# Sample selection of a two-layer hybrid decoder: row counts summed by a group matmul, and digits that carry the bias

## The chip, the cores and the metric

The kernel runs on one core of a Trainium2 chip. The core has five engines, each with an instruction queue of its own that it works through in the order in which it was written: PE (matrix multiplication; its weight loads are shown apart as PEld), DVE (vector), ACT (activation functions), POOL (a second vector engine, which also issues indirect transfers), and SP, which here only issues DMA transfers. Engines wait for one another by semaphores. SBUF is the on-chip memory of 128 partitions; PSUM is the memory into which PE writes its results, split into banks. The metric is the time of one execution on the device, in microseconds (us).

## What is computed

Two decoder layers run on a prompt of 1024 tokens and on 8 sample sequences of 4 new tokens with 2048 past keys each. In each layer one input projection feeds four groups of heads (a recurrent block, differential attention, sparse attention called DSA, and gated linear attention called GLA); an output projection and a gated MLP follow. The change is in DSA, in the choice of the 256 best-scored keys of each of the 32 sample tokens:

```python
def dsa_select(iq, iw, ik, q_pos, k_pos, topk):
    sc = jnp.einsum("bqhd,bsd->bqhs", iq, ik).astype(jnp.float32) * IDX_DIM ** -0.5
    score = jnp.einsum("bqh,bqhs->bqs", iw.astype(jnp.float32) * IDX_HEADS ** -0.5, jax.nn.relu(sc))
    score = jnp.where(k_pos[None, :] <= q_pos[:, None], score, -jnp.inf)
    val, idx = lax.top_k(score, topk)          # topk = 256
    return idx, jnp.isfinite(val)
```

## The kernel before, in words

The program is written layer by layer. A scheduler takes the instructions in the order in which the code emits them, simulates when they would run, and lays down one queue for each engine. On the chip these queues aren't reordered.

The stages of a layer that matter here are three. In the **dense stage** PE makes the input projections (L478) while DVE makes the threshold search of the prompt's own top-k (L833 to L906, tiles `tku`, `tkb`, `mk`). Then comes the **prelude** of GLA: a transfer brings the tile `ga`, PE multiplies it (L1823), ACT applies functions (L1824 to L1829), DVE makes a scan (L1830 to L1839) and the level tiles `gl` (L1885 to L1897), after which PE begins L1796. The **GLA stage** follows, with the differential attention of the samples (L1369, L1376, L1399) mixed in. DSA of the samples comes only behind it.

`sample_select()` finds, for each of 32 sample tokens, the 256th largest of 2176 scores. The scores of a token lie in four rows (partitions) of the tile `ss`, 128 rows of 544. The search fixes a threshold bit by bit. One **round** of it is: ACT applies Sign to all scores minus the candidate, and sums each row into `scnt` (L1017, an activation and a read of its accumulator); `group()` adds the counts of a token's four rows; DVE compares the sum with the number wanted (`sdf`, L1062), updates the threshold `sth` (L1063) and makes the next bias `snc` from it (L1059). There are 15 rounds on the upper 16 bits (`sdl`, L1037 to L1042), then `digits(15)` with 16 rounds on the lower bits, then `digits(12)` with 13 rounds on the position of equal scores; with three plain counts made by DVE (L1010) that makes 47 sums by `group()` in a layer. Between the two calls of `digits` a table is loaded by DMA (L1074) and combined with the scores (L1076).

The code is a generator. Each of its steps is emitted by others: in the dense stage by `background()`, once for each tile of a projection, in the GLA stage once for each second step of the GLA generator, and what is left by `samples()` before DSA:

```python
            while advance(ggen):
                n += KA
                count[0] += 1
                if count[0] % SELM == 0:
                    advance(sel)
                advance(sgen, int(n))
...
                while kind == "dsa" and advance(sel):
                    yield
```

PSUM is shared out by stage. `banks(**PSH)`, with PSH = dict(d=2,m=2,s=2), opens the banks of the dense stage; `banks(**PSG)` at L1748, with PSG = dict(d=2,e=1,g=5), closes `m` and `s` and opens `e` and `g` where they stood. `bank("m")` takes the next buffer of a tag. A tile in a bank that was another's waits until that one's readers are done.

Of the kernel before, what the change touches and what calls it, by code (L numbers as in the profile page):

```python
# [10 lines left out]
F32 = mybir.dt.float32  # L11
# [6 lines left out]
OP = mybir.AluOpType  # L18
# [53 lines left out]
def _const_tables():  # L72

    p = np.arange(128)
    c = {}
# [29 lines left out]
    pb, pj, pt = p // 16, (p // 4) % 4, p % 4  # L105
    bb, jj = np.arange(32) // 4, np.arange(32) % 4
    c["tailbad"] = ~((pj[:, None] == 3) & (pb[:, None] == bb[None, :]) & (jj[None, :] <= pt[:, None]))
    r = np.arange(32)
    c["agrp"] = ((p[:, None] % 32) // 16 == r[None, :] // 16) & (pt[:, None] == r[None, :] % 4)
    c["emat"] = np.concatenate([(pb[:, None] == b) & (pj[:, None] == p[None, :] // 32) & (pt[:, None] == p[None, :] % 4)  # L110
                                for b in range(8)], 1)
    c["newmask"] = np.concatenate([np.where((bb[None, :] == b) & (jj[None, :] <= pt[:, None]), 0.0, NEG)
# [3 lines left out]
    g, pp = np.arange(512) // 128, np.arange(512) % 128  # L116
# [18 lines left out]


CONST, COFF = _const_tables()


@with_exitstack  # L140
def trunk(ctx, tc, io, out, dbg=None, depth=DEPTH, stop=99):
    nc = tc.nc
    dve, act, pool, pe, sp = nc.vector, nc.scalar, nc.gpsimd, nc.tensor, nc.sync
    mult, add, sub = OP.mult, OP.add, OP.subtract
# [4 lines left out]
    psum = []  # L149

    def bank(tag="d"):
        pool_, bufs = psum[0 if tag in "de" else 1][:2]
        return pool_.tile([128, 512], F32, tag=tag, name=tag, bufs=bufs[tag])
# [62 lines left out]
    def const(key, dt=F32, where=None, parts=128, side="left"):  # L216
        o, w = COFF[key]
        t = (where or cp).tile([parts, w], dt, name="c_" + key, bufs=1)
        if dt == F32:
            sp.dma_start(t, cin[:parts, o:o + w])  # L220
        else:
            with tc.tile_pool(reuse_waits="tile", name="cs", bufs=1, side=side) as cs:
                s = cs.tile([parts, w], F32, name="cs_" + key)
                sp.dma_start(s, cin[:parts, o:o + w])
                pool.tensor_copy(t, s)
        return t
# [326 lines left out]
    with tc.tile_pool(reuse_waits="tile", name="xin", bufs=9) as xi:  # L553
# [6 lines left out]
        pc = bank("m")  # L560
        for k in range(8):
            pe.transpose(pc[:, 9 * k:9 * k + 9], c9[:, k * 128:k * 128 + 128], ident[:9, :9])
        th = xi.tile([128, 72], F32, name="th", bufs=1)
# [3 lines left out]
        for i, (t0, n) in enumerate(TOK):  # L567
            xn = xi.tile([128, D], F32, name="xn")
            sp.dma_start(xn[:n, :], xf_p[t0:t0 + 128, :] if i < 8 else xf_s)
            for q in range(2):  # L570
                pc = bank("d")
# [38 lines left out]
    pt = io["page_table"]  # L610
# [30 lines left out]
    for l in range(depth):  # L641
# [351 lines left out]
        def sample_select():  # L993
# [3 lines left out]

            def group(cnt):

                rep_ = kp.tile([128, 32], F32, name="srep", bufs=2)  # L1000
                dve.transpose(rep_, cnt.to_broadcast([128, 32]))
                pc = kp.tile([128, 1], F32, name="spc", bufs=2)
                dve.tensor_tensor_reduce(out=rep_, in0=rep_, in1=agrp, scale=1.0, scalar=0.0, op0=mult, op1=add,
                                         accum_out=pc)
                return pc

            def group_count(src, thr, op):

                cnt = kp.tile([128, 1], F32, name="scnt", bufs=2)
                dve.tensor_scalar(scs, src, thr, None, op0=op, op1=add, accum_out=cnt)  # L1010
                yield
                return group(cnt)

            def group_signs(src, bias, scale):

                cnt = kp.tile([128, 1], F32, name="scnt", bufs=2)
                act.activation(scs, src, AF.Sign, bias=bias, scale=scale, accum_out=cnt)  # L1017
                for _ in range(GY):
                    yield
                return group(cnt)  # L1020
# [7 lines left out]
            pc = yield from group_count(ss, 0.0, OP.is_ge)  # L1028
# [6 lines left out]
            for bit in range(30, 15, -1):  # L1035
                nc_ = kp.tile([128, 1], F32, name="snc", bufs=2)
                dve.tensor_scalar(nc_, cf, -1.0, cap[:, 0:1], op0=mult, op1=OP.min)  # L1037
                pc = yield from group_signs(hi16, nc_[:, 0:1], ng[:, 1:2])
                d = kp.tile([128, 1], I32, name="sdl", bufs=2)
                dve.tensor_scalar(d, pc, float(2 * TOPK - NS), float(1 << bit), op0=OP.is_lt, op1=mult)  # L1040
                dve.scalar_tensor_tensor(cs_, d, (1 << (bit - 1)) if bit > 16 else 0, cs_, op0=OP.bitwise_xor,
                                         op1=OP.bitwise_xor)  # L1042
            dve.tensor_scalar(cs_, cs_, -65536, None, op0=OP.bitwise_and)
            pc = yield from group_count(hi16, cf, OP.is_gt)
            need = kp.tile([128, 1], F32, name="sneed", bufs=1)
# [6 lines left out]
            th = kp.tile([128, 1], F32, name="sth", bufs=1)  # L1052
            dve.memset(th, 0.0)

            def digits(bits, need):

                for bit in range(bits, -1, -1):
                    nc_ = kp.tile([128, 1], F32, name="snc", bufs=2)
                    dve.tensor_scalar(nc_, th, -1.0, 0.5 - float(1 << bit), op0=mult, op1=add)  # L1059
                    pc = yield from group_signs(ev_, nc_[:, 0:1], 1.0)  # L1060
                    d = kp.tile([128, 1], F32, name="sdf", bufs=2)
                    dve.tensor_scalar(d, pc, need[:, 0:1], float(1 << bit), op0=OP.is_ge, op1=mult)  # L1062
                    dve.tensor_tensor(th, th, d, op=add)  # L1063

            yield from digits(15, need)
            lo = kp.tile([128, 1], I32, name="slo", bufs=1)
            dve.tensor_scalar(lo, th, ng[:, 2:3], ng[:, 3:4], op0=mult, op1=add)
            dve.tensor_tensor(cs_, cs_, lo, op=OP.bitwise_or)
            thr = cf
            pc = yield from group_count(ss, thr, OP.is_gt)  # L1070
# [138 lines left out]
        kp = kpool.__enter__()  # L1209
# [3 lines left out]
        agrp = const("agrp", where=kp)  # L1213
# [941 lines left out]
        if True:  # L2155
# [58 lines left out]
            for q in range(11):  # L2214
# [27 lines left out]
                for j in range(2):  # L2242
# [19 lines left out]
                    th = G[:, :T]  # L2262
# [99 lines left out]
```

## Time and profile before

| | us |
|---|---|
| median of 3 runs (lowest, highest) | 3806.49 (3804.55, 3810.34) |
| the profiled execution | 3821.09 |
| its span, first to last instruction | 3819.3 |
| mean granted clock of TensorE in it | 0.956 |

The profile shows one execution. A share of busy time is a mean over all stages: PE is busy for 91% of the span and DVE for 64%, but the search is in use only from 377 to 684 us in layer 0 and from 2255 to 2550 us in layer 1, so it is the stretches there that are to be read, one by one.

### The profile page before, as it was taken

The page shows a single profiled execution, that of the slowest core. Times are in us where ns is not written, and L with a number is a line of the kernel's source. Part 1 is how long each engine was busy: PE and PEld are TensorE (multiplying, and loading weights), DVE is VectorE, ACT ScalarE, POOL GpSimd, SP SyncE. Part 2 cuts the span into 40 slices and gives each one's busy share as a digit, 9 for nine tenths or more (in the row PEclk, how much of TensorE's full clock was granted, in tenths as well). Part 3 has the DMA queues.
Part 4 walks back from the last instruction along what each step waited for, and adds up shares of the span by engine and source line. Part 5 has one row for each costly group of instructions (what it writes and reads, how often), then busy time and mean ns, then how long its engine had stood idle before and what let it go on. Part 6 is the DMA issues. An engine that isn't in the chain of part 4 may idle for free.

```text
span 3819.3 us, 64298 instructions
## 1 busy us (share of the span) xinstructions
PE 3494.2 (91%) x24916; PEld 3125.7 (82%) x24916; DVE 2452.0 (64%) x5724; ACT 1500.7 (39%) x3026; POOL 1271.7 (33%) x1179
## 2 busy tenths in 40 slices
PE   7999868899899999999989988588997999999998
PEld 4888855576699999999979877356666999999997
DVE  5479998677554444455564999986763645555555
ACT  4445643476532121212244557436663322122122
POOL 2134146534333222222322521654333233222231
PEclk8999979999999999999989999699998999999999
DMA  6453345646511432321123332456455011111111
GB/s 232 136 158 107 96 125 167 204 144 206 181 44 49 116 103 73 94 78 45 45 83 95 104 96 70 135 177 201 154 170 175 28 40 56 45 45 45 45 51 52
DMA packets 351404, 407.64 MB, mean 107 GB/s; under 512 B 93712, under 2 KB 299262, under 8 KB 349915
## 3 DMA queue, kind: packets, MB, share of 16 engines
q1 hardware_dynamic: 312186, 265.09, 23.0%
q0 software_dynamic: 38912, 138.43, 10.9%
q8 instruction: 197, 3.23, 0.4%
q14 instruction: 109, 0.89, 0.1%
HBM read 354.32 MB, written 58.04 MB: 108 GB/s over the span
## 4 chain that ended last, share of the span: by engine, by line
PE 68%; DVE 19%; DMA 4%; issue 4%; ACT 3%; POOL 1%; SPq 1%; another core or an unknown queue 0%; DVEq 0%; ACTq 0%; POOLq 0%
PE d L478 31%; PE m L2180 13%; PE d L498 4%; PE d L1369 3%; DVE tku L833 3%; DVE tkb L833 2%; PE e L1399 2%; PE e L1376 1%; PE m L1637 1%; PE d L330 1%; PE m L1696 1%; DVE ny L413 1%; PE g L1796 1%; PE m L753 1%; PE m L1689 1%
## 5 line engine op out<-in xcount | busy, mean ns | idle before, releaser
L478 PE MATMUL d<-h,wh 128*128 128x384 f32 (+1 forms) x5856 | 1405.7, 326 | 52.4 <-ACT h L468 15.7
L478 PEld LDWEIGHTS d<-h,wh 128*128 128x128 f32 x5856 | 1030.3, 190 | 67.7 <-ACT te L706 16.2
L478 PE MATMUL d<-h,wl 128*128 128x384 f32 (+1 forms) x2928 | 945.2, 325 | 8.5 <-POOL wl L462 8.5
L478 PEld LDWEIGHTS d<-h,wl 128*128 128x128 f32 x2928 | 556.4, 190 | 13.4 <-POOL wl L462 12.0
L498 PE MATMUL d<-wh,h 128*128 128x256 f32 (+1 forms) x2304 | 450.3, 291 | 34.3 <-ACT nat L697 16.1
L507 DVE SCALAR_TENSOR_TENSOR xT<-m,mod,xT 128x384 f32<-128x384 f32 (+1 forms) x480 | 273.1, 572 | 228.7 <-PE m L2180 227.8
L498 PEld LDWEIGHTS d<-wh,h 128*128 128x128 f32 (+1 forms) x2304 | 360.3, 186 | 56.3 <-ACT nat L697 19.6
L462 POOL TENSOR_TENSOR wl<-wr,wh 128x1024 fp32r<-128x1024 f32 (+1 forms) x124 | 259.8, 2112 | 310.3 <-ACT wh L461 244.3
L2180 PE MATMUL m<-mh,wdh 128*128 128x384 f32 (+1 forms) x1056 | 350.4, 332 | 0.4 <-DVE xT L507 0.4
L2180 PE MATMUL m<-ml,wdh 128*128 128x384 f32 (+1 forms) x1056 | 344.0, 326 | 0.0
L2180 PE MATMUL m<-mh,wdl 128*128 128x384 f32 (+1 forms) x1056 | 341.9, 325 | 0.0
L498 PE MATMUL d<-wl,h 128*128 128x256 f32 (+1 forms) x1152 | 333.5, 290 | 3.1 <-DVE wl L462 2.0
L2279 POOL TENSOR_TENSOR ml<-z,mh 128x384 fp32r<-128x384 f32 x132 | 132.9, 1026 | 599.8 <-ACT mh L2278 599.8
L461 ACT CAST wh<-wr 128x1024 fp32r<-128x1024 f32 (+1 forms) x172 | 158.2, 956 | 210.7 <-PE d L478 172.3
L2250 DVE COPY fs<-G 128x2 f32<-128x2 f32 x44 | 50.8, 1156 | 278.4 <-ACT G L2230 278.4
L2230 ACT COPY G<-d 128x384 f32<-128x384 f32 x132 | 57.3, 442 | 421.6 <-PE d L478 393.8
L498 PEld LDWEIGHTS d<-wl,h 128*128 128x128 f32 (+1 forms) x1152 | 214.5, 186 | 7.7 <-issue 2.6
L2180 PEld LDWEIGHTS m<-mh,wdh 128*128 128x128 f32 x1056 | 200.0, 189 | 9.1 <-issue 6.7
L2180 PEld LDWEIGHTS m<-ml,wdh 128*128 128x128 f32 x1056 | 200.2, 190 | 1.4 <-issue 0.9
L2180 PEld LDWEIGHTS m<-mh,wdl 128*128 128x128 f32 x1056 | 200.0, 189 | 0.0
L2170 POOL TENSOR_TENSOR wdl<-wr,wdh 128x1024 fp32r<-128x1024 f32 x44 | 104.9, 2416 | 263.9 <-ACT wdh L2169 263.9
L1369 PE MATMUL d<-c_ident,kv 128*128 128x128 f32 x1024 | 167.0, 291 | 16.3 <-ACT KT L210 7.7
(556 smaller groups left out, 6600.2 us busy)
## 6 DMA issues: line engine op xcount, KB each, us to landing
adaw<-in_w_ada_dram SPq DMA_DIRECT2D x80, 512.0 KB
wr<-in_w_in_dram SPq DMA_DIRECT2D x48, 512.0 KB
wr<-in_ffn_w_gate_dram SPq DMA_DIRECT2D x44, 512.0 KB
wr<-in_ffn_w_up_dram SPq DMA_DIRECT2D x44, 512.0 KB
wr<-in_ffn_w_down_dram SPq DMA_DIRECT2D x44, 512.0 KB
xd<-xT SPq DMA_DIRECT2D x16, 528.0 KB
adaw<-in_w_ada_dram SPq DMA_DIRECT2D x8, 1024.0 KB
wr<-in_w_out_dram SPq DMA_DIRECT2D x32, 256.0 KB
```

Source lines behind the costliest of these rows:

```text
L461: act.copy(hi[:, ks, :width], raw[:, :, :width])
L462: eng.tensor_tensor(lo[:, ks, :width], raw[:, :, :width], hi[:, ks, :width].bitcast(F32), op=sub)
L478: pe.matmul(pd, lhsT=w[a][:, k, j * 128:j * 128 + 128], rhs=h[b][c][:, k, :], start=(q == 0), stop=(q == 23))
L498: pe.matmul(pd[:n, :256], lhsT=h[b][c][:, k, t0:t0 + n], rhs=w[a][:, k, :], start=(q == 0), stop=(q == 23))
L507: dve.scalar_tensor_tensor(x[:, m, t0:t0 + n], p[:, :n], mod[:, gate + m, 0:1], x[:, m, t0:t0 + n], op0=mult, op1=add)
L833: dve.tensor_scalar(scratch[:, :n], src[:, s], thr[:, j:j + 1], None, op0=OP.is_ge, op1=add, accum_out=cnt[:, j:j + 1])
L1369: pe.transpose(pm[:, z_ * 128:z_ * 128 + 128], kg[:, j, f * 128:f * 128 + 128], ident)
L1399: pe.matmul(po[32 * j:32 * j + 32, :256], lhsT=wT[:, g, 32 * j:32 * j + 32], rhs=vg[:, j, :], start=(g == 0), stop=(g == 3))
L2170: pool.tensor_tensor(lo[:, z_, :], raw, hi[:, z_, :].bitcast(F32), op=sub)
L2180: pe.matmul(pd, lhsT=a, rhs=b, start=(n == 0), stop=(n == len(ops) - 1))
L2230: act.copy(Gp[:, 2 + CHK[c][0]:2 + CHK[c][0] + n], p[:, :n])
L2279: pool.tensor_tensor(ml[:, cs], z[:, cs], mh[:, cs].bitcast(F32), op=sub)
```

## The change

`group()` no longer transposes the counts and reduces them under a mask on DVE; PE multiplies the counts `scnt` by a 128x128 matrix of zeros and ones (`agrp`, which grows from 32 to 128 columns) into a PSUM bank, tag `m` while the dense stage's banks are open, else `g`. The comparisons read the sum from PSUM. In `digits` the bias itself is carried from round to round: `sdf` and a scalar_tensor_tensor that writes the next `snc`, two DVE operations instead of three; the threshold `sth` is made from it once at the end. The rounds on the upper bits (L1036 to L1042) keep their three operations.

```diff
     bb, jj = np.arange(32) // 4, np.arange(32) % 4
     c["tailbad"] = ~((pj[:, None] == 3) & (pb[:, None] == bb[None, :]) & (jj[None, :] <= pt[:, None]))
     r = np.arange(32)
-    c["agrp"] = ((p[:, None] % 32) // 16 == r[None, :] // 16) & (pt[:, None] == r[None, :] % 4)
+    c["agrp"] = (p[:, None] // 16 == p[None, :] // 16) & (pt[:, None] == p[None, :] % 4)
     c["emat"] = np.concatenate([(pb[:, None] == b) & (pj[:, None] == p[None, :] // 32) & (pt[:, None] == p[None, :] % 4)
                                 for b in range(8)], 1)
     c["newmask"] = np.concatenate([np.where((bb[None, :] == b) & (jj[None, :] <= pt[:, None]), 0.0, NEG)
...
@@ -997,11 +997,8 @@
 
             def group(cnt):
 
-                rep_ = kp.tile([128, 32], F32, name="srep", bufs=2)
-                dve.transpose(rep_, cnt.to_broadcast([128, 32]))
-                pc = kp.tile([128, 1], F32, name="spc", bufs=2)
-                dve.tensor_tensor_reduce(out=rep_, in0=rep_, in1=agrp, scale=1.0, scalar=0.0, op0=mult, op1=add,
-                                         accum_out=pc)
+                pc = bank("m" if "m" in psum[1][1] else "g")[:, :1]
+                pe.matmul(pc, lhsT=agrp, rhs=cnt, start=True, stop=True)
                 return pc
 
             def group_count(src, thr, op):
@@ -1054,13 +1051,18 @@
 
             def digits(bits, need):
 
+
+                nc_ = kp.tile([128, 1], F32, name="snc", bufs=2)
+                dve.memset(nc_, 0.5 - float(1 << bits))
                 for bit in range(bits, -1, -1):
-                    nc_ = kp.tile([128, 1], F32, name="snc", bufs=2)
-                    dve.tensor_scalar(nc_, th, -1.0, 0.5 - float(1 << bit), op0=mult, op1=add)
                     pc = yield from group_signs(ev_, nc_[:, 0:1], 1.0)
+                    step = 0.5 * float(1 << bit)
                     d = kp.tile([128, 1], F32, name="sdf", bufs=2)
-                    dve.tensor_scalar(d, pc, need[:, 0:1], float(1 << bit), op0=OP.is_ge, op1=mult)
-                    dve.tensor_tensor(th, th, d, op=add)
+                    dve.tensor_scalar(d, pc, need[:, 0:1], -2.0 * step, op0=OP.is_ge, op1=mult)
+                    nx = kp.tile([128, 1], F32, name="snc", bufs=2)
+                    dve.scalar_tensor_tensor(nx, d, step, nc_, op0=add, op1=add)
+                    nc_ = nx
+                dve.tensor_scalar(th, nc_, -1.0, None, op0=mult)
 
             yield from digits(15, need)
             lo = kp.tile([128, 1], I32, name="slo", bufs=1)
```

Where the scheduler now puts the work, on two engines. First PE at the end of the dense stage of layer 0. The rows are in queue order, each with its line, operation, out<-in and shape; `x` counts rows in a row. Before, the last projection (L478) is followed at once by the multiplication of `ga`:

```order
L478 MATMUL d<-h_489,wh 128x288
L478 MATMUL d<-h_490,wl 128x288
L1823 MATMUL g<-ga,wa_6437 128x256 x2
L1911 MATMUL g<-c_ident,gke 128x128
L1319 MATMUL d<-c_ident,s_q 128x32
L1320 MATMUL d<-c_ident,s_k 128x32
L1319 MATMUL d<-c_ident,s_q 128x32
```

In the changed kernel the group matmuls of the search stand between (lines shift by two: L1825 is L1823 of before):

```order
L478 MATMUL d<-h_489,wh 128x288
L1001 MATMUL m<-scnt,c_agrp 128x1
L478 MATMUL d<-h_490,wl 128x288
L1001 MATMUL m<-scnt,c_agrp 128x1 x22
L1321 MATMUL d<-c_ident,s_q 128x32
L1322 MATMUL d<-c_ident,s_k 128x32
L1321 MATMUL d<-c_ident,s_q 128x32
L1322 MATMUL d<-c_ident,s_k 128x32
L1001 MATMUL g<-scnt,c_agrp 128x1
L1825 MATMUL g<-ga,wa_6335 128x256 x2
```

Twenty-two of them follow each other with nothing between, and `ga` stands behind them. Of the 47 group matmuls of this layer 41 write tag `m` and 6 tag `g`. Layer 1 is alike:

```order
L478 MATMUL d<-h_19715,wl 128x288
L1001 MATMUL m<-scnt,c_agrp 128x1 x3
L1194 MATMUL m<-c_ident,so_rows 36x128 x2
L1001 MATMUL m<-scnt,c_agrp 128x1 x23
L1321 MATMUL d<-c_ident,s_q 128x32
```

There 3 and 23 stand behind the last projection, and the next of other stages stands behind these.

Second DVE, from the last instruction of the prompt's top-k (`mk`, L906) on. Before, the GLA prelude (L1830 on) follows, and a round's five operations are spread over it, one to three rows at a time:

```order
L906 TENSOR_SCALAR mk<-tkb 128x1024
L1059 TENSOR_SCALAR snc<-sth 128x1
L1830 SCALAR_TENSOR_TENSOR gla<-gla,gex 128x512
L1832 TENSOR_SCALAR gla<-gla 128x512
L1001 STREAM_TRANSPOSE srep<-scnt 128x32
L1839 SCALAR_TENSOR_TENSOR gb<-grm,gla 128x512
L1003 ISA srep,spc<-srep,c_agrp 128x32
L1003 ISA spc 128x1
L1885 TENSOR_TENSOR gl_6593<-gb 128x4x64
L1885 TENSOR_TENSOR gl_6608<-gb 128x8x32
```

In the changed kernel the prelude is not there; after two rows that prepare `cvec` come the pairs `sdf` and `snc` of the rounds:

```order
L906 TENSOR_SCALAR mk<-tkb 128x1024
L1063 SCALAR_TENSOR_TENSOR snc<-sdf,snc 128x1
L1277 TENSOR_TENSOR cvec<-c_m_435,nlam 128x1
L1278 TENSOR_TENSOR cvec<-cvec,c_m_433 128x1
L1061 TENSOR_SCALAR sdf<-m,sneed 128x1
L1063 SCALAR_TENSOR_TENSOR snc<-sdf,snc 128x1
L1061 TENSOR_SCALAR sdf<-m,sneed 128x1
L1063 SCALAR_TENSOR_TENSOR snc<-sdf,snc 128x1
```

These pairs go on, twelve in all; then come the end of `digits(15)`, the count and the table, and the first of seven more pairs:

```order
L1061 TENSOR_SCALAR sdf<-m,sneed 128x1
L1063 SCALAR_TENSOR_TENSOR snc<-sdf,snc 128x1
L1065 TENSOR_SCALAR sth<-snc 128x1
L1056 MEMSET snc 128x1
L1069 TENSOR_SCALAR slo<-sth,sng 128x1
L1070 TENSOR_TENSOR scand<-scand,slo 128x1
L1079 MEMSET sth 128x1
L1007 TENSOR_SCALAR selb,scnt<-ss,scand 128x544
L1078 SCALAR_TENSOR_TENSOR sev<-ss,scand,sev 128x544
L1073 TENSOR_SCALAR sneed<-m 128x1
L1061 TENSOR_SCALAR sdf<-m,sneed 128x1
```

So 12 + 1 + 7 = 20 rounds stand in a row on DVE; in layer 1 it is 14 + 1 + 7 = 22. On ACT the same rounds stand as one block of 20 activations, ahead of the functions of the GLA prelude (L1826):

```order
L1014 ACTIVATE selb,scnt<-sev,snc 128x544 x2
L1273 ACTIVATE ls<-ls 128x2
L1857 ACTIVATE gq<-gq 128x512
L1014 ACTIVATE selb,scnt<-sev,snc 128x544 x20
L1324 COPY s_qT<-d 128x64
L1326 COPY s_kT<-d 128x64
L1826 ACTIVATE gla<-g,V 128x256 x2
```

The 20 activations had other work between them before.

## Rows read from the trace of the kernel before

**Rows 1.** First part of the page: busy time of each engine.

```profile
PE 3494.2 (91%) x24916; PEld 3125.7 (82%) x24916; DVE 2452.0 (64%) x5724; ACT 1500.7 (39%) x3026; POOL 1271.7 (33%) x1179
```

**Rows 2.** Windows: busy us PE, PEld, DVE, ACT, POOL, then TensorE clock, DMA.

```profile
375.00:521.00 146.00, 127.77 (x867) 120.23 (x865) 144.55 (x456) 91.59 (x178) 26.33 (x19) 0.96 0.29 93
521.00:556.00 35.00, 4.92 (x40) 3.44 (x39) 34.18 (x93) 14.86 (x29) 19.79 (x24) 0.57 0.61 154
556.00:690.00 134.00, 116.84 (x783) 79.47 (x781) 113.88 (x334) 52.08 (x108) 87.53 (x118) 0.88 0.49 155
```

**Rows 3.** Timeline of PE, layer 0: start, length, [idle <-releaser].

```profile
520.84 0.29 PE L478 MATMUL d<-h,wl 128*128 128x288 f32 x1
532.32 2.04 PE L1823 MATMUL g<-ga,wa 16*128 16x256 f32 x4 [11.19 <-DMA ga<-stt_a]
...
558.82 1.06 PE L1796 MATMUL g<-gbd,gl 128*128 128x256 f32 x2
```

**Rows 4.** Timeline of PE, layer 1.

```profile
2393.07 1.19 PE L1823 MATMUL g<-ga,wa 16*128 16x256 f32 x2 [12.56 <-DMA ga<-stt_a]
```

**Rows 5.** Timeline of DVE, layer 0: last threshold pass of the top-k.

```profile
505.57 0.60 DVE L898 TENSOR_SCALAR_CACHE_REDUCE tkb<-sc,cand 128x384 bf16<-128x384 f32 x1
...
538.92 0.41 DVE L906 TENSOR_SCALAR mk<-tkb 128x1024 bf16<-128x1024 bf16 x1
...
539.32 0.68 DVE L1830 SCALAR_TENSOR_TENSOR gla<-gla,gex 128x512 f32<-128x512 f32 x1
```

**Rows 6.** Timeline of ACT, layer 0.

```profile
537.51 0.63 ACT L1829 ACTIVATE gex<-gex 128x512 f32<-128x512 f32 x1
```

**Rows 7.** Timeline of DVE, layer 1.

```profile
2381.67 0.61 DVE L898 TENSOR_SCALAR_CACHE_REDUCE tkb<-sc,cand 128x384 bf16<-128x384 f32 x1
...
2435.09 0.41 DVE L906 TENSOR_SCALAR mk<-tkb 128x1024 bf16<-128x1024 bf16 x1
```

**Rows 8.** Timeline of all engines, one round in the GLA stage.

```profile
650.20 0.22 DVE L1062 TENSOR_SCALAR sdf<-spc,sneed 128x1 f32<-128x1 f32 x1
...
650.45 0.16 DVE L1063 TENSOR_TENSOR sth<-sth,sdf 128x1 f32<-128x1 f32 x1
...
651.36 0.15 DVE L1059 TENSOR_SCALAR snc<-sth 128x1 f32<-128x1 f32 x1
...
651.61 0.75 ACT L1017 ACTIVATE selb<-sev,snc 128x544 bf16<-128x544 f32 x1 [2.45 <-DVE snc L1059]
...
652.27 0.19 ACT L1017 ACTIVATION_READ_ACCUMULATOR selb<-sev,snc 128x1 f32 x1
...
652.49 0.21 DVE L1001 STREAM_TRANSPOSE srep<-scnt 128x32 f32<-128x32 f32 x1 [0.97 <-ACT selb L1017]
```

**Rows 9.** Lines L340 and L342: durations ns min/median/max, first and last start.

```profile
L340 PEld LDWEIGHTS m<-c_sum,adae x192: 186/192/337, 40.5 to 1703.2; 128*128 128x128 f32 x192
L340 PE MATMUL m<-c_sum,adae x192: 171/257/363, 40.5 to 1703.2; 128*128 128x9 f32 x192
...
L342 DVE TENSOR_TENSOR mod<-m,V x24: 178/194/197, 41.6 to 1703.8; 128x36 f32<-128x36 f32 x24
```

**Rows 10.** Timeline of all engines, layer 1: the table between the two searches.

```profile
2473.97 0.33 SPq L1074 DMA_DIRECT2D sev<-in_const_dram  x1
...
2477.65 0.78 DVE L1076 SCALAR_TENSOR_TENSOR sev<-ss,scand,sev 128x544 f32<-128x544 f32 x1
```

**Rows 11.** Groups of DVE in the GLA stage, layer 0: busy us, mean ns.

```profile
L1003 DVE CUSTOM_DVE_ANT_0 srep<-srep,c_agrp 128x32 f32<-128x32 f32 x22 | 7.3, 333 | 0.2
L1063 DVE TENSOR_TENSOR sth<-sth,sdf 128x1 f32<-128x1 f32 x22 | 6.0, 274 | 0.3
L1001 DVE STREAM_TRANSPOSE srep<-scnt 128x32 f32<-128x32 f32 x22 | 4.5, 206 | 4.3 <-ACT selb L1017 4.0
...
L1059 DVE TENSOR_SCALAR snc<-sth 128x1 f32<-128x1 f32 x21 | 3.1, 150 | 0.2
```

**Rows 12.** Chain that ended last in 556:690, by line.

```profile
by line: PE g L1796 17.3%; PE d L1369 9.2%; DVE gatt L1807 7.1%; PE e L1376 6.4%; PE e L1399 5.3%; issue 4.2%; PE g L1921 4.0%; DVE gS L1980 3.0%; PE g L1953 2.8%; PE g L1920 2.8%; ACT selb L1017 2.5%; DVE gS L1928 2.4%; POOL kv L245 2.1%; 
```

## The prediction

> **What bounds the kernel now.** I read the page first, then windows around the search, then the timelines at the end of the dense stage, and last the chain of waits of the GLA stage. The page [rows 1] gives PE 91% of the span, but that is a mean over stages, and the search lives in few of them. The windows [rows 2] show three different limits in layer 0. From 375 to 521 DVE is the bound: it is busy for 144.55 of 146 us, PE for 127.77. From 521 to 556 PE does almost nothing (4.92 of 35 us, clock 0.57), and DVE works on alone (34.18 us). From 556 to 690 PE leads again (116.84 of 134 us at 0.88), with DVE at 113.88.
>
> What PE waits for between 521 and 556 is in the timelines. Its last projection starts at 520.84; it then idles 11.19 us for the transfer of `ga` and multiplies it at 532.32; the stage really starts with L1796 at 558.82 [rows 3]. ACT has its part of the prelude done at 537.51 + 0.63 = 538.14 [rows 6], so from `ga` on that took 5.8 us. DVE is later: its last top-k instruction ends at 538.92 + 0.41 = 539.33, and the prelude's first operation L1830 starts at 539.32 [rows 5]. So here DVE's backlog sets the start of the GLA stage, and everything that DVE has to do before L1830 moves it one for one. In layer 1 `ga` is multiplied at 2393.07 [rows 4], in the middle of the last top-k pass (2381.67 to 2435.50 [rows 7]); that pass takes 53.8 us against 539.33 − 505.57 = 33.8 us in layer 0 [rows 5, 7], because the prelude is threaded into it.
>
> **What the change does to order.** The queues printed above are facts that need no run: behind the last projection PE has 22 group matmuls in a row in layer 0 and 23 in layer 1, DVE has 20 and 22 whole rounds ahead of L1830, ACT one block of 20. A round is a closed loop: the next Sign needs the bias made from the last count. So nothing in that block overlaps with itself, and the engines that are in it have nothing else that they are allowed to do: `ga`'s multiplication stands behind the matmuls on PE, the GLA functions behind the activations on ACT, the scan behind the pairs on DVE. Before, these rounds ran in gaps between GLA work; now they stand in series with it.
>
> The Trainium skill says the same of the queues (PSUM — Partial Sum Buffer, Engine vs sequencer instructions): ScalarE's and VectorE's are strict FIFO, and matmuls start and complete in program order. It speaks against the change. The trace bears it out in that PE did nothing else in the 11.19 us in which it waited for `ga` [rows 3]. Were waiting matmuls passed by later ones, the stretch would cost PE nothing and only DVE's and ACT's queues would hold the prelude.
>
> **The price of a round there.** From rows 8: the bias starts 0.25 us before the Sign that it releases (651.36 to 651.61); the Sign and its read end 0.85 us later (652.27 + 0.19 − 651.61); the next engine starts 0.03 us behind (652.49). The comparison `sdf` and the operation after it start 0.25 us apart (650.20 to 650.45), and I take the scalar_tensor_tensor to be like that one. The group matmul isn't in the trace. The nearest is L340, fp32, weights 128x128, nine columns [rows 9]: a weight load of 0.19 us (0.34 at most), a matmul of 0.26 (0.36 at most). From below, if the weights are already in when the count arrives, 0.26; from above, an exposed load and two passes at the slowest, 0.34 + 2 × 0.36 = 1.06. PE idles and its clock was 0.57 in such a stretch, so I take the middle, 0.66. With 0.05 us from PE to DVE, an estimate by the 0.03 above: 0.25 + 0.85 + 0.03 + 0.66 + 0.05 + 0.25 = 2.09, say **2.1 us**, between 1.7 and 2.5.
>
> What reading PSUM adds is small by the trace: L342 reads a bank on DVE in 0.19 us [rows 9], and `sdf` from SBUF takes 0.22 [rows 8], so I add nothing. The Trainium skill (Perfetto Trace Analysis, Optimizing Scalar/DVE Operations) gives DVE about 60 ns of overhead on SBUF and 125 ns on PSUM; by it the 94 sums would cost 94 × 0.065 = 6 us more, an estimate, and the forecast would be 3 us higher for the 42 in series. The row decides.
>
> **The sum.** Dense stage first: a round in it loses transpose, reduce, read and one small operation on a saturated DVE. By rows 11 transpose and reduce occupy 0.21 and 0.33 us in busy time; starts lie closer than ends, so I count 0.3 us, times 22 rounds: 7 us earlier. Bounds 0 (PE now waits inside the dense stage for DVE's counts and gives it back) and 14 (0.21 + 0.33 + 0.08, all of it exposed).
>
> Layer 0: top-k ends at 539.3 − 7 = 532.3. Twenty rounds, 42 us. The table between them is loaded into `sev`, which the Signs read, so its transfer can't start before the last of sixteen; in layer 1 L1076 followed 3.68 us behind the issue and took 0.78 [rows 10]. With the count beside it I take 4 us. That is 578.3. Then `ga` to the end of ACT's part, 5.8, and from L1830 to L1796 before it was 19.5 us [rows 3, 5], with some search between, so 17: 601.1, against 558.8 before. **+42 us**.
>
> Layer 1: 2381.7 − 7 + 33.8 (the pass without the prelude, as in layer 0) = 2408.5; 22 rounds, 46.2, and 4: 2458.7; plus 5.8 and 17: 2481.5. Before, DVE had pass and prelude behind it at 2435.5. **+46 us**.
>
> Given back: these rounds are no longer in the GLA stage. DVE spent 7.3 + 6.0 + 4.5 + 3.1 us there on four of their operations, with `sdf` (22 × 0.22 [rows 8]) and the rest some 30 us of 113.88 [rows 2, 11]. But the chain of that stage is PE's first; of the search it holds the Sign by 2.5% (3.3 us of 134) and a few of its DVE operations [rows 12]. PE is busy for 116.84 of 134 us, so no more than 17 us is to be had at that clock. I take 12 us a layer, between 3 and 25.
>
> +42 + 46 − 24 = **+64 us**. Against the profiled execution, 3819.3 of span and 1.8 around it, that is 3885; against the median of the runs, which is 14.6 lower, 3806.5 + 64 = **3870 us**.
>
> Edits costed at nothing: the wider constant `agrp` (loaded once, long before use); the memset and the closing negation of `digits`, four small DVE instructions in all; that the search ends earlier (it ended at about 684 and 2550 and nothing waited for it). If PE's clock is still low when the stage begins, the first L1796 pay for it; they did so before too.
>
> **The rivals.**
> - *Most is given back.* PE is 87% busy in the GLA stage, but part of that is waiting drawn as busy; with DVE relieved of 30 us and the clock back at its upper level the stage could shrink by 25 us a layer. With rounds at 1.9 us, 4 us less in each layer, and a dense gain of 10, 3 us more: 35 + 39 − 50 = +24, 3830 us. Against it: L1796 and L1369, both PE, lead the chain [rows 12].
> - *The dense stage stalls too.* Group matmuls stand between projections there (one is in the rows printed). Each makes PE wait for a count that a saturated DVE delivers late. Some 34 rounds of both layers at about 1 us: +98, 3904 us. For it: DVE has no slack there [rows 2]. Against it: PE has 18 us of slack in 146.
> - *Faster.* The GLA stage is bound by DVE after all, and each us taken off it shortens the stage. With a round at its floor of 1.7 us and a dense gain of 14, the layers stand at 42 − 7 − 8 = +27 and 46 − 7 − 9 = +30; giving back the whole 30 us in both, and the 3.3 us of Sign on the chain too, makes −10, some 3797 us. It decides from 28.5 us a layer on. That needs PE's 116.84 us to fit in 101 to 105, about what a clock of 1.0 for 0.88 would make of them (103). Against it: 113.88 of 134 us for DVE is not a full engine, and everything must go right at once. The Trainium skill (same page and section) holds that work taken off a saturated DVE may make sense; the trace has DVE saturated in the dense stage, not in the GLA stage.
> - *No change.* The stretch is hidden by something that I don't see, a late `ga` or another late transfer. Before, `ga` was there at 532.32 [rows 3], 45 us ahead of where the block ends, so I give this little.
>
> **Numbers.** Forecast 0.68 (its own range 3842 to 3902), most given back 0.14, dense stage too 0.10, faster 0.04, no change 0.04. Two runs of this kernel tell apart about 0.2%, 7.6 us. Slower 0.92, same 0.04, faster 0.04. The range goes from 3828, which takes in the dearer half of the second case, to 3906, the price of the third.
>
> **What would show it.** In the changed trace: between the last projection and L1825 only L1001 on PE, some 20 of them, about 2.1 us apart, clock near half; L1830's successor on DVE at about 584 instead of 539; ACT with a Sign in each 2.1 us and nothing else. The GLA stage behind it 12 us shorter, with hardly any `sdf`. A dense stage that ends 5 to 7 us earlier on DVE. It would be wrong if rounds take 3 us or more (then PE to DVE hand-overs are dear), if the block is short because most rounds are over when the top-k ends, or if the GLA stage shrinks by over 25 us a layer.

## The result, and the profile after

The changed kernel took 3895.25 us (median of 4 runs, 3890.8 to 3907.2); the kernel before, beside it, 3807.07 us (3804.55 to 3810.34). The ratio is 1.0231, 95% interval 1.0215 to 1.0247: 88 us slower. Forecast were 3870 us and a loss of 64.

The profiled execution took 3890.8 us, at the lower end of the runs, while the one of before stood 14 us above its median; so the two profiles differ by only 70 us, and stages are compared below by the places where both have the same work. The engines first, in answer to [rows 1]:

```profile
PE 3518.8 (90%) x25104; PEld 3150.9 (81%) x25104; DVE 2421.5 (62%) x5392; ACT 1503.7 (39%) x3026; POOL 1273.9 (33%) x1179
```

DVE does 30.5 us less, in 332 fewer instructions; PE 24.6 us more, in 188 more matmul records, two for each of 94 group sums. Less work on DVE, and the kernel is longer by 69.7 us of span: PE's idle time grew by 45.1 us (370.2 for 325.1), so most of the loss is waiting. PE's timeline (start, length, [idle <-releaser]) from the last projection of layer 0 to the first L1798, which is L1796 of before, answers to [rows 3]:

```profile
525.75 0.38 PE L478 MATMUL d<-h,wl 128*128 128x288 f32 x1
531.52 0.58 PE L1001 MATMUL m<-scnt,c_agrp 128*128 128x1 f32 x2 [5.39 <-ACT selb L1014]
538.85 0.59 PE L1001 MATMUL m<-scnt,c_agrp 128*128 128x1 f32 x2 [6.75 <-ACT selb L1014]
...
549.96 0.58 PE L1001 MATMUL m<-scnt,c_agrp 128*128 128x1 f32 x2 [1.53 <-ACT selb L1014]
552.08 0.59 PE L1001 MATMUL m<-scnt,c_agrp 128*128 128x1 f32 x2 [1.53 <-ACT selb L1014]
554.19 0.58 PE L1001 MATMUL m<-scnt,c_agrp 128*128 128x1 f32 x2 [1.53 <-ACT selb L1014]
...
581.99 0.58 PE L1001 MATMUL m<-scnt,c_agrp 128*128 128x1 f32 x2 [1.53 <-ACT selb L1014]
...
584.62 2.07 PE L1825 MATMUL g<-ga,wa 16*128 16x256 f32 x4
...
614.47 1.91 PE L1798 MATMUL g<-gbd,gl 128*128 128x256 f32 x4
```

Between 525.75 and 584.62 PE does nothing but L1001 and four small transposes, and from 543 on waits some 1.5 us for a Sign nearly each time. `ga` is multiplied at 584.62 (before 532.32), and the GLA stage starts at 614.47 (before 558.82): 55.6 us late. One round in the middle, all engines:

```profile
553.30 0.75 ACT L1014 ACTIVATE selb<-sev,snc 128x544 bf16<-128x544 f32 x1 [1.28 <-DVE snc L1063]
553.96 0.19 ACT L1014 ACTIVATION_READ_ACCUMULATOR selb<-sev,snc 128x1 f32 x1
554.19 0.50 PEld L1001 LDWEIGHTS m<-scnt,c_agrp 128*128 128x128 f32 x2 [1.61 <-ACT selb L1014]
554.19 0.58 PE L1001 MATMUL m<-scnt,c_agrp 128*128 128x1 f32 x2 [1.53 <-ACT selb L1014]
554.82 0.22 DVE L1061 TENSOR_SCALAR sdf<-m,sneed 128x1 f32<-128x1 f32 x1 [1.63 <-PE m L1001]
555.14 0.16 DVE L1063 SCALAR_TENSOR_TENSOR snc<-sdf,snc 128x1 f32<-128x1 f32 x1
555.42 0.75 ACT L1014 ACTIVATE selb<-sev,snc 128x544 bf16<-128x544 f32 x1 [1.27 <-DVE snc L1063]
```

From Sign to Sign it is 2.12 us: 0.89 to the matmul, 0.63 from there to `sdf`, 0.32 to the next bias, 0.28 to the next Sign. The windows (us PE, PEld, DVE, ACT, POOL, then clock, DMA), in answer to [rows 2]: dense stage, block, prelude, GLA stage.

```profile
375.40:521.40 146.00, 127.89 (x877) 120.06 (x876) 140.06 (x384) 88.57 (x170) 24.37 (x19) 0.98 0.27 88
540.00:583.00 43.00, 12.16 (x44) 10.52 (x44) 10.12 (x53) 15.97 (x38) 6.62 (x10) 0.50 0.47 127
584.60:614.50 29.90, 18.93 (x121) 13.29 (x122) 23.63 (x61) 17.58 (x34) 12.75 (x16) 0.61 0.24 74
614.50:742.70 128.20, 116.08 (x858) 75.32 (x858) 93.05 (x206) 36.87 (x70) 90.12 (x120) 0.93 0.56 180
```

In the block no engine is busy for even 40% of the time, and the granted clock is 0.50, the 1.2 GHz level. DVE's own landmarks answer to [rows 5]:

```profile
540.02 0.45 DVE L906 TENSOR_SCALAR mk<-tkb 128x1024 bf16<-128x1024 bf16 x1
...
591.08 0.69 DVE L1832 SCALAR_TENSOR_TENSOR gla<-gla,gex 128x512 f32<-128x512 f32 x1
```

The last top-k instruction ends at 540.47 (before 539.33), the prelude begins at 591.08 (before 539.32). Fifty us between two instructions that stood next to each other.

### The profile page after: what moved, and what is told of

Read it like the earlier page. It is cut to its first block, busy times and chain, and to the rows that moved or that the text cites. A ratio compares the mean times of both kernels' runs of the same rounds, so it can differ in the third digit from the quotient of the medians.

```text
span 3889.0 us, 64419 instructions
## 1 busy us (share of the span) xinstructions
PE 3518.8 (90%) x25104; PEld 3150.9 (81%) x25104; DVE 2421.5 (62%) x5392; ACT 1503.7 (39%) x3026; POOL 1273.9 (33%) x1179
## 4 chain that ended last, share of the span: by engine, by line
PE 67%; DVE 17%; ACT 5%; issue 5%; DMA 4%; POOL 1%; SPq 1%; another core or an unknown queue 0%; DVEq 0%; ACTq 0%; POOLq 0%
PE d L478 31%; PE m L2182 13%; PE d L498 4%; PE d L1371 2%; DVE tku L833 2%; DVE tkb L833 2%; PE e L1401 2%; PE g L1798 1%; PE e L1378 1%; PE d L330 1%; PE m L1639 1%; DVE ny L413 1%; ACT selb L1014 1%; PE m L1698 1%; PE m L753 1%
## 5 line engine op out<-in xcount | busy, mean ns | idle before, releaser
L478 PE MATMUL d<-h,wh 128*128 128x384 f32 (+1 forms) x5856 | 1408.0, 326 | 40.0 <-ACT h L468 17.8
L478 PEld LDWEIGHTS d<-h,wh 128*128 128x128 f32 x5856 | 1030.8, 190 | 54.5 <-ACT h L468 18.3
L478 PE MATMUL d<-h,wl 128*128 128x384 f32 (+1 forms) x2928 | 946.5, 326 | 8.4 <-POOL wl L462 8.4
L478 PEld LDWEIGHTS d<-h,wl 128*128 128x128 f32 x2928 | 557.1, 191 | 12.9 <-POOL wl L462 11.3
L498 PE MATMUL d<-wh,h 128*128 128x256 f32 (+1 forms) x2304 | 444.7, 289 | 20.3 <-ACT rraw L693 6.2
L462 POOL TENSOR_TENSOR wl<-wr,wh 128x1024 fp32r<-128x1024 f32 (+1 forms) x124 | 260.5, 2119 | 310.6 <-ACT wh L461 232.6
```

Source lines behind the costliest of these rows:

```text
L462: eng.tensor_tensor(lo[:, ks, :width], raw[:, :, :width], hi[:, ks, :width].bitcast(F32), op=sub)
L478: pe.matmul(pd, lhsT=w[a][:, k, j * 128:j * 128 + 128], rhs=h[b][c][:, k, :], start=(q == 0), stop=(q == 23))
L498: pe.matmul(pd[:n, :256], lhsT=h[b][c][:, k, t0:t0 + n], rhs=w[a][:, k, :], start=(q == 0), stop=(q == 23))
```

## The experiments

All times are compared with runs of the kernel before on the same chip. That kernel took 3804 us beside the first four runs and 3783 us beside the others, which ran on other chips, so ratios are compared, not times. Expectations in us are to be read with that: they were made for 3804.

**One half of the change at a time.** The first kernel is before with the new `digits` alone, the second before with the new `group()` alone:

```diff
 first (e1): group() as before
-                    dve.tensor_scalar(nc_, th, -1.0, 0.5 - float(1 << bit), op0=mult, op1=add)
+                    dve.scalar_tensor_tensor(nx, d, step, nc_, op0=add, op1=add)
...
 second (e2): digits() as before
-                dve.transpose(rep_, cnt.to_broadcast([128, 32]))
...
+                pe.matmul(pc, lhsT=agrp, rhs=cnt, start=True, stop=True)
```

> Before, with only the second half of the change: digits carry the bias, the counts are still summed by transpose and reduce on DVE. Block theory (the loss is the 20 and 22 rounds that stand in series ahead of the GLA prelude, because the group matmuls write banks of tag m that the GLA stage's banks replace): no matmul, no block, so no loss; one DVE operation fewer in each of 58 rounds is worth at most 58 x 0.15 = 9 us: 3797 to 3810 us, ratio 0.997 to 1.001. Rival (carrying the bias makes the chain of a round longer or places it worse): some part of the 88 us stays, over 3830 us.

> Before, with only the first half: group matmul, old digits with three DVE operations. Its PE queue has 23 group matmuls in a row at the end of the dense stage of both layers. Block theory: as the changed kernel, with each round in the block 0.25 us longer (one DVE step more): 3895 + 42 x 0.25 = 3905 us, 3893 to 3920. Rival (the bias form brings a good part of the loss): clearly under 3880.

Measured: 1.0041 (1.0027 to 1.0055) for the bias alone, 1.0313 (1.0296 to 1.0331) for the matmul alone. The matmul alone costs more than the whole change. The bias alone missed its expectation on the other side: 16 us slower where up to 9 us were to be gained. In the table below no one stage carries it: the GLA stage of layer 0 is 4 us longer than in both profiles of before, and layer 1 up to the end of its GLA stage 4 to 7 us. The rounds of the second kernel's block, on DVE and ACT:

```profile
561.46 0.15 DVE L1056 TENSOR_SCALAR snc<-sth 128x1 f32<-128x1 f32 x1
561.73 0.75 ACT L1014 ACTIVATE selb<-sev,snc 128x544 bf16<-128x544 f32 x1 [1.46 <-DVE snc L1056]
...
564.03 0.75 ACT L1014 ACTIVATE selb<-sev,snc 128x544 bf16<-128x544 f32 x1 [1.47 <-DVE snc L1056]
```

The period is 2.30 us, 0.18 more than in the changed kernel; 40 digit rounds make 7 us of it. The kernel was 119 us slower where 101 were expected, 3 us above the range.

**A bank of its own.** The changed kernel, with the group matmuls writing a bank that is opened ahead of the dense stage's and closed behind the GLA stage's; a run of before with the same smaller tags is its measure:

```diff
-PSH = dict(d=2,m=2,s=2)
-PSG = dict(d=2,e=1,g=5)
+PSH = dict(d=2,m=1,s=2)
+PSG = dict(d=2,e=1,g=4)
...
-                pc = bank("m" if "m" in psum[1][1] else "g")[:, :1]
+                pc = (ownp.tile([128, 512], F32, tag="o", name="o", bufs=1) if own else bank("m"))[:, :1]
...
```

> The changed kernel, but the group matmuls write one PSUM bank of their own that lives through the dense and the GLA stage; to make room tag m has 1 buffer for 2 in the dense stage and g 4 for 5 in the GLA stage. Its PE queue has at most 4 group matmuls in a row. Block theory: the loss is gone but for what the smaller tags cost: 3795 to 3830 us. Rival 1 (a small matmul waiting in PE's queue is dear wherever it stands): 94 sums still wait on PE, over 3850. Rival 2 (the block comes from elsewhere): as changed, 3895.

> The kernel before with the smaller tags alone (m 1 for 2, g 4 for 5), as the measure for the run with a bank of its own. No theory speaks of it: 3800 to 3830 us. If it is over 3850, the smaller tags cost much, and the run with its own bank must be read against this one.

Measured: 1.0109 (1.0090 to 1.0129) with its own bank, 1.0085 (1.0063 to 1.0106) for the smaller tags alone. Both times, 3844 and 3838 us, lie above what was expected: the smaller tags were dearer (33 us). Against them the group matmul with the new digits costs 0.2%, and the intervals overlap: within the noise the loss is gone but for what the tags cost. PE at the end of the dense stage of the kernel with its own bank:

```profile
531.50 0.29 PE L478 MATMUL d<-h,wl 128*128 128x288 f32 x1
534.36 0.38 PE L1005 MATMUL o<-scnt,c_agrp 128*128 128x1 f32 x2 [2.56 <-ACT selb L1018]
540.27 0.59 PE L1005 MATMUL o<-scnt,c_agrp 128*128 128x1 f32 x2 [5.53 <-ACT selb L1018]
545.35 0.59 PE L1005 MATMUL o<-scnt,c_agrp 128*128 128x1 f32 x2 [4.50 <-ACT selb L1018]
547.40 0.59 PE L1005 MATMUL o<-scnt,c_agrp 128*128 128x1 f32 x2 [1.46 <-ACT selb L1018]
547.92 2.07 PE L1829 MATMUL g<-ga,wa 16*128 16x256 f32 x4
```

Four rounds, then `ga` at 547.92 and not at 584.62. The same 94 sums wait on the same PE; what is gone is their common tag with the banks that the GLA stage replaces, and with it the block.

**Making a round longer.** Each Sign of a lower-digit round is made twice, in the changed kernel and in the one before:

```diff
+                if src is not hi16:
+                    act.activation(scs, src, AF.Sign, bias=bias, scale=scale)
                 act.activation(scs, src, AF.Sign, bias=bias, scale=scale, accum_out=cnt)
```

> The changed kernel with each Sign of the lower-digit rounds made twice (the first one's result is overwritten, the second is the one that counts). Starts of Sign and of the read behind it lie 0.66 us apart. Block theory: the 40 digit rounds in the block are in series with everything, so the kernel is longer by 40 x 0.66 = 26 us, 3921 us, between 3910 and 3940. Rival (the loss comes from PE stalls spread over the dense and the GLA stage, rounds being hidden): under 3905.

> The kernel before with the same second Sign. There the rounds run beside other work and ACT is busy for 39% of the span, so most of 58 x 0.66 = 38 us is hidden: 3804 + 0 to 12 us. If the kernel before gets longer by over 25 us, the rounds are on its path too, and the block isn't what makes the difference.

Measured: 1.0350 (1.0333 to 1.0367) against 1.0231, that is 0.0119 x 3783 = 45 us longer; the kernel before 1.0022 (1.0012 to 1.0032), 8 us longer. The same work costs five times as much in the changed kernel. ACT in the block:

```profile
562.53 0.75 ACT L1015 ACTIVATE selb<-sev,snc 128x544 bf16<-128x544 f32 x1 [1.25 <-DVE snc L1065]
563.31 0.75 ACT L1016 ACTIVATE selb<-sev,snc 128x544 bf16<-128x544 f32 x1
563.96 0.19 ACT L1016 ACTIVATION_READ_ACCUMULATOR selb<-sev,snc 128x1 f32 x1
565.40 0.75 ACT L1015 ACTIVATE selb<-sev,snc 128x544 bf16<-128x544 f32 x1 [1.25 <-DVE snc L1065]
```

The period went from 2.12 to 2.87 us: 0.75, not the 0.66 that I had taken from the distance of a Sign and its read, since two Signs start 0.78 apart. 40 x 0.75 = 30 us; 15 us more than that were measured. The two profiles are of different chips, but the block can be compared: from the end of the top-k to `ga` it took 59.7 us in layer 0 (44.2 in the changed kernel) and 66.3 in layer 1 (47.2), 35 us more. Up to the first L1796 the two layers are longer by 44 us; behind it each GLA stage is 14 us shorter, with the samples' attention placed otherwise, so the rest of the 15 can't be put down to one place.

**Fewer rounds in the block.** SELH sets for each how many-th projection tile `background()` emits a round (2 here, 4 in a third run); rounds that the dense stage doesn't emit fall into the GLA stage and write tag `g`:

```diff
-SELH = 1
+SELH = 2
```

> The changed kernel with one number changed: the dense stage emits a round of the search for each second projection tile (SELH 2 for 1). 54 of 94 group matmuls then write tag g in the GLA stage, and PE has 7 and 10 in a row at the end of the dense stages, for 22 and 23. Block theory: the loss shrinks with the rounds that are left in the block, 17 x 2.1 = 36 us of 88: 3840 us, between 3810 and 3855. Rival (94 waiting matmuls are dear wherever they stand): over 3870.

> The kernel before with the same number changed, as the measure for the run above. The dense stage of DVE loses some 11 rounds of its 22, the GLA stage gains them: 3790 to 3830 us; no theory speaks of it.

> The changed kernel with SELH 4: one round of the search for each fourth projection tile. 76 of 94 group matmuls write tag g in the GLA stage; no more than 3 stand in a row at the end of a dense stage. Theory 1 (only rounds in a row cost): with 3 left, the ratio to before is 0.998 to 1.004. Theory 2 (a group matmul also costs in the GLA stage, since it takes a buffer of the ring g, which others then wait for, and holds PE's queue; by the run with SELH 2, whose GLA stage was 18 us longer with 27 such rounds): 35 rounds a layer make about 1.010 to 1.015, no better than SELH 2, which had 1.0099.

Measured: 1.0099 (1.0083 to 1.0116) with SELH 2, 0.9992 (0.9981 to 1.0003) for before with SELH 2, 1.0060 (1.0042 to 1.0078) with SELH 4. With SELH 2 that is 3842 us where the kernel before takes 3804, as the block theory has it. The loss falls with the group matmuls of tag `m` that PE has in a row behind the last projection, both layers together: 45 of them 0.0231, 17 of them 0.0099, and with SELH 4, where the trace has one in layer 0 and three in layer 1, 0.0060. The last lies between the expectations of both theories: the block is most of the loss, and some 0.6% remains almost without it. A table of stages, each length worked out from PE's timeline (start of L986, the samples' scores; first and last L1796; last L1696, the prompt's attention), shows where:

| layer 0, us | L986 to first L1796 | first to last L1796 | to last L1696 | layer 1: L986 to last L1796 |
|---|---|---|---|---|
| before | 188.7 | 126.3 | 327.5 | 307.0 |
| before, second profile | 187.8 | 125.4 | 315.2 | 304.5 |
| changed | 244.1 | 128.2 | 317.2 | 365.1 |
| bias alone | 187.6 | 129.8 | 322.5 | 311.1 |
| matmul alone | 251.9 | 127.0 | 318.2 | 372.6 |
| own bank | 195.8 | 120.7 | 334.9 | 323.7 |
| before, smaller tags | 197.2 | 138.0 | 323.7 | 322.0 |
| SELH 2 | 216.7 | 136.7 | 303.1 | 345.5 |
| SELH 4 | 202.5 | 143.3 | 298.4 | 336.5 |
| before, SELH 2 | 188.6 | 118.8 | 317.8 | 302.6 |
| two Signs | 263.8 | 113.9 | 315.5 | 375.5 |
| before, two Signs | 187.5 | 130.9 | 314.4 | 302.1 |
| hybrid | 187.2 | 145.6 | 322.8 | 303.6 |
| bias, SELH 2 | 187.1 | 128.7 | 311.4 | 304.2 |

With SELH 4 the GLA stage of layer 0 begins 15 us later than in the second profile of before and is 18 us longer, and the attention behind it is 17 us shorter. Not all of that is the search. The last `gl` tile of the prelude and the first L1798, from DVE's and PE's timelines of this run:

```profile
555.81 0.41 DVE L1899 TENSOR_TENSOR gl<-gl,gk 128x256 f32<-128x256 f32 x1
...
566.44 1.11 PE L1798 MATMUL g<-gbd,gl 128*128 128x256 f32 x4
```

The tile is ready 192.3 us behind L986, against 186.1 in the kernel before; with SELH 2 it is 203.3, in the changed kernel 241.4. So the prelude of layer 0 is late by 55, 17 and 6 us with 22, 7 and one matmuls in the row. What the two SELH kernels lose beyond that until L1798 starts (13 and 10 us, against 2.6 before and 2.7 in the changed kernel) is matmuls of the samples' attention and of the search that stand ahead of it in PE's queue. And the loss that SELH 4 leaves is not waiting. Its page, behind that of the second profile of before:

```profile
PE 3480.6 (92%) x24916; PEld 3120.9 (83%) x24916; DVE 2457.5 (65%) x5724; ACT 1502.4 (40%) x3026; POOL 1270.4 (34%) x1179
```

```profile
PE 3501.2 (92%) x25104; PEld 3140.6 (83%) x25104; DVE 2430.2 (64%) x5392; ACT 1503.9 (40%) x3026; POOL 1275.9 (34%) x1179
```

PE is busy for 20.6 us more, and the span is 20.3 us longer (3800.1 for 3779.8), so PE idles no more than before; the group matmuls are busy for 33.7 us, part of it beside other matmuls. In the two GLA stages PE waits for the search for 1.0 and 3.6 us, too little for what theory 2 reckons with. One profile of each kernel reads so; no run varied it.

**Matmul in the GLA stage only**, in a bank of its own there, transposes in the dense stage; and the bias form with SELH 2:

```diff
 hybrid (e7), beside the new digits and SELH = 2
-PSG = dict(d=2,e=1,g=5)
+PSG = dict(d=2,e=1,g=4,o=1)
...
+                if "o" in psum[1][1]:
+                    pc = bank("o")[:, :1]
+                    pe.matmul(pc, lhsT=agrm, rhs=cnt, start=True, stop=True)
+                    return pc
...
```

> Digits carry the bias, SELH 2; the sum is made by transpose and reduce on DVE while the dense stage's banks are open, and by matmul into a bank of its own (tag o) in the GLA stage, where g has 4 buffers for 5. 54 matmuls, at most 4 in a row, none of them in a ring that others use. Theory 2: no block and no shared ring, DVE relieved in the GLA stage; what is left is the price of g 4 for 5: ratio 0.993 to 1.004. Theory 3 (a matmul that waits for a count holds PE's queue in the GLA stage, whatever bank it writes): 1.006 or more.

> Only the bias form of the digits, as in the first run, but with SELH 2, where the kernel before measured 0.9992. If the 1.0041 of the first run came from the bias form itself, 1.003 to 1.005 here too; if it came from how that one arrangement of instructions fell, 0.997 to 1.001.

> The kernel before, unchanged, for a second profile of it: the first one stands 14 us above the median of its runs. All theories: ratio 1.000, and if the profile falls near the median, it shows in which stage the first one was longer.

Measured: the hybrid 1.0074 (1.0058 to 1.0091). By the expectation that favours theory 3: a matmul that holds PE's queue whatever it writes. But the table warns: the prelude is on time (187.2), and layer 0's GLA stage is 145.6 us long, as `g` with 4 buffers alone made it 138.0 in the kernel before, while the kernel with its own bank and the same 4 buffers has 120.7, and layer 1 of the hybrid is not late at all (303.6). In its two GLA stages PE waits for counts for 1.9 and 5.8 us, of 28 us by which this profile is longer than the second one of before; 10 of the 28 lie between the layers, from the last L1696 of layer 0 to L986 of layer 1, where no search runs. So theory 3 isn't shown, and what the matmul costs in the GLA stage stays open.

The bias form with SELH 2 came to 0.9975 (0.9966 to 0.9985): 0.25% below the kernel before, and within what was expected if the 1.0041 of the first run belongs to one arrangement of instructions and not to the bias form. What in that arrangement costs 0.4% stays open. The second profile of before ended at 3781.6 us, at its median; it differs from the first in layer 0 by 12 us in the attention behind the GLA stage and by 1 us in each of the two stretches ahead of it. In layer 1 the stretch up to the end of the GLA stage differs by 2.5 us. The argument rests on these stretches, which repeat.

## Why the prediction was right, and where its sizes were off

**The mechanism.** It was the forecast's own: rounds in series between the last projection and `ga`, DVE's prelude behind them, the kernel slower. The time, 3895, lies in the range, and the loss is 24 us above the one forecast. What the prediction took from the queues alone (20 rounds ahead of L1830) happened as printed. That the common PSUM tag is what puts them there was not in it; the run with its own bank showed it.

**The round.** 2.12 us, forecast 2.1. The matmul's part from the count to `sdf` is 0.04 + 0.63, forecast 0.03 + 0.66 + 0.05. The step from `sdf` to the next bias was 0.32, not 0.25, so carrying the bias saves 0.18 of a round, not 0.25. Reading PSUM cost nothing that shows: `sdf` took 0.22 us from a bank, as from SBUF [rows 8]. The rule of the Trainium skill (Perfetto Trace Analysis, Optimizing Scalar/DVE Operations) that DVE has about 125 ns of overhead on PSUM for 60 on SBUF doesn't show in this operation. The other rule of the Trainium skill cited ahead, that matmuls start in program order (PSUM — Partial Sum Buffer, Engine vs sequencer instructions), does: `ga`'s multiplication started at 584.62, behind the last group matmul that stands ahead of it, at 584.10.

**The dense gain failed.** I counted 7 us a layer of DVE's relief. In layer 0 the top-k ended 1.1 us later than before. DVE did get lighter there, 140.06 us in 146 for 144.55 [rows 2], but up to the end of the top-k it idled 5 us more than before. PE waited in its queue for counts (engine line waited for: us, times, longest):

```profile
PE m L1001 <- ACT selb L1014: 8.6, 7, 3.0
```

Before, PE had no wait for counts in this stretch. But it had 15 us of waits for `nat`, `rraw` and `te`, of which 2 are left, so that its idle time hardly changed, 18.7 us for 18.3. The last projection came 4.9 us late because PE was busy for 132.0 us up to its end, 127.9 before; the group matmuls are 6.7 us of the 132.0, and the prediction counted no such work on PE for the dense stage. In layer 1 the last projection came 0.8 us earlier, counted from L986. The bound of 0 for the gain was the truth. Its reason, PE's waits, is shown in part only: PE idles no longer than before, but 2.9 us of DVE's new idle time is a wait for ACT's `lth`, whose matmuls (L1147) waited 1.9 us, by the profile, for the search's `sdl`, which reads banks of the same tag `m`.

**The block and the prelude.** From the end of the top-k to `ga`: 44.2 us, forecast 46. From `ga` to L1832 6.5, forecast 5.8. From there to L1798 23.4, forecast 17: three rounds, three copies of the samples' `KT` and steps of their softmax run in it on DVE. With the 8 us of the dense gain this is the whole of the difference in layer 0, +55.6 for +42. In layer 1 the block, from 2457.85 to `ga` at 2505.04, took 47.2 us for 50.2 forecast.

**Layer 1 was counted from the wrong place.** The prediction took 2435.5, the end of the pass, as the point from which its +46 counts. But before, PE began L1796 17 us earlier, inside the pass. The first L1796 of layer 1 before, and in the changed kernel:

```profile
2418.82 1.22 PE L1796 MATMUL g<-gbd,gl 128*128 128x256 f32 x2 [1.34 <-POOL gbd L1789]
```

```profile
2532.53 1.47 PE L1798 MATMUL g<-gbd,gl 128*128 128x256 f32 x4
```

From L986 on this is 169.9 us before and 237.3 now, 67 us later; the forecast's 2481.5 is 232.6 from there, so where the stage would start was right to 5 us, and what it was compared with was not. The two starts together came 123 us later, where 88 were forecast.

**Given back: the mis-sized term with the wrong place.** Forecast were 12 us a layer in the GLA stage. In layer 0 that stage went from 126.3 to 128.2 us. DVE was relieved, 93.05 us of 128.20, and the stage didn't care. In its place PE did more there; the matmuls of the samples' differential attention in this stage, before and after:

```profile
L1376 PE MATMUL e<-KT,s_Q 128*32 128x256 f32 x128 | 14.9, 469 | 6.2 <-ACT KT L210 4.8 <-DVE spc L1003 1.4
L1399 PE MATMUL e<-kv,s_wT 128*32 128x256 f32 x107 | 9.4, 397 | 0.0
```

```profile
L1401 PE MATMUL e<-kv,s_wT 128*32 128x256 f32 x160 | 17.9, 432 | 0.0
L1378 PE MATMUL e<-KT,s_Q 128*32 128x256 f32 x144 | 12.3, 413 | 5.8 <-DVE KT L212 4.5 <-ACT s_ob L1403 1.4
```

160 instead of 107 of one kind, 144 instead of 128 of the other: the samples' attention moved forward into the GLA stage. Its next step, L1439, came only 19 us later than before (717.2 for 698.4) while the end of the GLA stage came 57.6 later. Some of that head start came back behind it, in the prompt's attention, 317.2 us for 327.5 in the first profile of before, but only 315.2 in the second, so for layer 0 how much is not certain. In layer 1 more was given back, most of it in that attention: its GLA stage took 127.8 us (137.1 in the first profile of before, 132.9 in the second), the prompt's attention behind it 304.8 (332.7 and 324.4), together 25 to 37 us. The loss came out 24 us above the forecast although the starts alone were 35 us above it: the difference came back in a place where nothing was forecast, and that much is luck. The chain of layer 0's GLA stage names a second reason:

```profile
by line: PE g L1798 19.9%; PE d L1371 10.3%; PE e L1401 10.2%; DMA gk<-stt_gla_k 5.2%; DMA ggg<-stt_gla_g 4.4%; issue 4.0%; PE e L1378 3.6%; PE g L1922 3.3%; PE g L1977 3.3%; PE g L1955 3.1%; PE g L1923 2.8%; PE g L1926 2.6%; PE d L1392 2.2
```

Transfers of `gk` and `ggg` stand in it with 5.2 and 4.4%, 12 us; they are not among the lines of [rows 12]. Whether those 12 us could have been had, no run tried.

**The rivals.** That most is given back in the GLA stage is refuted by its length in layer 0 and by 5 to 9 us, not 25, in layer 1. Faster and no change are out by the ratio. The dense stage that stalls too had the price, 3904, that is nearest to the time measured, but its mechanism isn't there: the last projection is 4.9 us late in layer 0 and not at all in layer 1; 34 us were reckoned for both.

## What to carry to other kernels

Moving a small sum from one engine to another also moves its result to another memory, and the buffers there have owners: a PSUM tag that the next stage replaces ties the last of its readers to the first of the next stage. Look in the new queues, before any run, for a closed loop that stands in a row with nothing between; its period times its count is the length of the block, and here that was right to 3 us in both layers. What the kernel loses by it is another sum: work that other engines do in the meantime comes back later. And a relief of a stage's second engine is worth what its first engine has to wait for: here 20 us of DVE bought nothing in the GLA stage of layer 0. In a kernel whose PE is busy for 91% of the span, a matmul is not free either.

## What was not expected

A one-column fp32 matmul with a 128x128 weight took 0.59 us at the granted clock of 0.50, and 0.63 us until DVE read it; at the end of the dense stage (519.63, in a window with clock 0.98) it took 0.38. At the lower clock that is no shorter than the way that it replaces: in the kernel before 0.48 us passed from a transpose to the `sdf` behind it (652.49 to 652.97). There a round gains nothing by the matmul. Two Signs of 128x544 start 0.78 us apart where a Sign and the read of its sum start 0.66 apart. One PSUM buffer fewer for tag `m` in the dense stage and one fewer of five for `g` in the GLA stage cost 33 us together. The same kernel took 3804 and 3783 us on different chips.
